# Two layers of a hybrid decoder in fp32 precision on one core: a list scheduler's cost model and priorities are changed

## The chip, the cores and the metric

One core of a Trainium2 chip. The time is that of one execution on the device, in microseconds (us); a run is given by the median of its executions. TensorE multiplies matrices into PSUM (8 banks), VectorE, ScalarE and GpSimd work on SBUF tiles, and SP issues all DMAs. In rows of the profile PE is TensorE (PEld its weight loads), DVE is VectorE, ACT is ScalarE, POOL is GpSimd, and SPq is the queue of SP.

## The reference

Two layers over x of 512 tokens by 1024 channels, float32. In each layer one input projection feeds four mixers, whose outputs (256 channels each) go through one output projection; then a LayerNorm, an MLP and a second LayerNorm.

```python
for l in range(DEPTH):                       # 2
    h = x @ w_in[l]
    (a_qkv, a_a, a_b, a_z, b_cq, b_ckv, b_kr, c_q, c_f, c_i, c_g, d_qkv) = split(h)
    o_a = _gated_deltanet(...)     # A: conv, L2 norm, chunks of 64, inverse of a unit triangular
                                   #    matrix per chunk, a state carried over 8 chunks, gated RMSNorm
    o_b = _mla(...)                # B: low-rank q and kv (RMSNorm), rotary key, causal softmax
    o_c = _hgrn2(...)              # C: forget gates, cumulative decays, outer-product state
    o_d = _dilated_attention(...)  # D: causal softmax with a bias table per head
    mixed = concat([o_a, o_b, o_c, o_d]) @ w_out[l]
    x = _layer_norm(ALPHA * x + mixed, ln1_g[l], ln1_b[l])
    x = _layer_norm(ALPHA * x + square(relu(x @ w_ff1[l])) @ w_ff2[l], ln2_g[l], ln2_b[l])
```

## The kernel before, in words

Everything stays transposed (channels on partitions, 512 tokens along the free dimension). A dense product is done in three TensorE matmuls of a reduced fp32 format (`mm3`): each operand is split into a high part (ScalarE, `split`) and the rest (VectorE), and high x high, high x low and low x high are added in PSUM. Weights come by DMA as `wr` (128x1024), and `wh` and `wl` are their two parts; activations are `xH`/`xL`, the mixers' outputs `mixH`/`mixL`, the MLP's `hH`/`hL`. A tile of the input projection is 24 dense matmuls of 512 columns. Small products (chunks of A and C, scores, transposes) are plain fp32 and use a part of the array: 64x64, 64x32, 32x32, 128x64 or 64x128 rows by columns of weights. Each such matmul leaves two records in the trace, a transpose one.

The program is written stage by stage, and each stage has a stream name: A, A0 and A1 (the two head pairs of A), B, C, C0 and C1, D, O (output projection, `w_out`, in three groups of mixer outputs) and F (MLP). Nothing is issued as it is written. `Plan.record` takes each instruction with its engine, what it depends on (`deps`, with a flag for a true read after write), a cost from `cost`, its tiles and a priority: its place in the program, less `bias`, plus `BIAS` of its stream and engine. `Plan.order` is a list scheduler: it keeps a clock per engine, and takes again and again the instruction that can start soonest by these costs; of those on one engine that can start equally soon the one of the lowest priority number. TensorE has more rules: it models the granted clock from its own activity (`WINDOW`, `DOWN`, `UP`), a price for leaving and entering a tile shape (`LEAVE`, `ENTER`), and it prefers dense matmuls while a running mean of activity (`EMA`) lies under `FILL`. Tiles are taken from pools of fixed size (41 rows of 128x512, 8 PSUM banks, 2 `wr`, 5 `wh`, 5 `wl`); `wr`, `wh` and `wl` go in the order of the program, and the dense accumulators (`mm`) hold at most 5 banks. `emit` then issues the instructions in that order, engine by engine; all have the line of `emit`'s loop, L472.

Names that the steps speak of. A: `LT` is the triangular matrix, `X`, `LB`, `W` and `TB` the steps of its inverse (15 pairs of `W` and `TB`, each pair reading the last), `Z` and then `U` and `T` the inverse put back by transposes; `a<-T,N` is TensorE's first use of it. `ke` and `ktok` are keys in token order, `vn` and `st` the state. B: `sqh`/`sql` are the two parts of a square whose sum over channels TensorE takes, `qh`/`kh` queries and keys, `at`/`as` the softmax of one head, `btab` its table. C: `kr`, `qa`, `sc`, `kt`, `vt`, `sn`. D: `dq`, `dk` and `dl` (high and low parts), `dtab` its four tables; its softmax is `at`/`as` too, and `tt` the transposed result. O: `xt` are the eight tiles of x, loaded before the first group (`load_x`) and added to on VectorE.

## Time and profile before

| | us |
|---|---|
| median of three runs | 1382.39 |
| lowest, highest | 1381.54, 1384.11 |
| the profiled execution | 1383.82 |
| its span, first to last instruction | 1382.0 |
| mean granted TensorE clock | 0.985 |
| TensorE, VectorE, ScalarE, GpSimd busy | 1336.3, 784.7, 596.6, 91.4 |

The span is what the page and the trace show; the execution takes 1.8 us more. A busy TensorE is not TensorE at its peak: its matmuls overlap, and the ends of their records are modelled, so the time from start to start is what a matmul costs in a row of them. A granted clock of 1.00 is 2.4 GHz, 0.50 is 1.2 GHz. The two layers lie at 0 to 690 us and 690 to 1382 us; in each, the mixers take the first half and the MLP the second.

### The profile page before, as it was taken

To read this page: it belongs to the slowest core of one execution; us is meant where nothing else is said; L and a number is where in the kernel's file an instruction comes from. 1 tells how busy PE (TensorE), PEld (TensorE's weight loads), DVE (VectorE), ACT (ScalarE), POOL (GpSimd) and SP (SyncE) were. 2 spreads that over 40 slices of the span, in tenths; PEclk is the share of its full clock that TensorE was granted. 3 is DMA by queue.
4 is the path that set the end of the run, shared out by engine and by line. 5 is a ranking of instruction groups with operands and counts; after the bars stand their busy time and mean duration, and the time that the engine had idled before them with its cause. 6 is when DMAs were issued, how large, how long until landed. Compare 5 with 4: busy or idle time off the path is not lost.

```text
span 1382.0 us, 21797 instructions
## 1 busy us (share of the span) xinstructions
PE 1336.3 (97%) x8860; PEld 1084.0 (78%) x8860; DVE 784.7 (57%) x1533; ACT 596.6 (43%) x1124; POOL 91.4 (7%) x108
## 2 busy tenths in 40 slices
PE   8899999999999999999998989999999999999997
PEld 7657778778888888888886678787788888888886
DVE  6989585567743334422479898846658333344226
ACT  6643456548432223321485434656374322233112
POOL 0222020010000000000003212200000000000000
PEclk9999999999999999999999999999999999999999
DMA  6122201232542223324122242021415323232341
GB/s 225 40 88 77 82 4 47 77 122 74 165 141 93 92 92 94 105 92 155 59 92 62 92 146 71 3 69 69 135 64 189 116 92 92 92 106 92 126 149 61
DMA packets 44164, 132.65 MB, mean 96 GB/s; under 512 B 4896, under 2 KB 5152, under 8 KB 44064
## 3 DMA queue, kind: packets, MB, share of 16 engines
q1 hardware_dynamic: 44064, 131.27, 29.5%
q8 instruction: 69, 1.13, 0.3%
q14 instruction: 31, 0.25, 0.1%
HBM read 122.86 MB, written 8.39 MB: 95 GB/s over the span
## 4 chain that ended last, share of the span: by engine, by line
PE 76%; DVE 14%; ACT 7%; issue 2%; DMA 1%; POOL 0%; SPq 0%; DVEq 0%; POOLq 0%; ACTq 0%
PE mm L472 42%; PE a L472 17%; PE b L472 16%; ACT lny L472 2%; DVE wl L472 1%; DVE xt L472 1%; DVE y L472 1%; ACT wh L472 1%; DVE vtok L472 1%; PE o L472 1%; DVE ktok L472 1%; ACT scr L472 1%; ACT sg L472 1%; ACT xH L472 1%; DVE X L472 1%
## 5 line engine op out<-in xcount | busy, mean ns | idle before, releaser
L472 DVE TENSOR_TENSOR wl<-wr,wh 128x1024 fp32r<-128x1024 f32 (+1 forms) x195 | 237.6, 1222 | 360.4 <-ACT wh L472 355.1
L472 ACT ACTIVATE wh<-wr 128x1024 fp32r<-128x1024 f32 (+1 forms) x195 | 204.7, 1054 | 528.6 <-PE mm L472 501.1
L472 PE MATMUL mm<-xH,wl 128*128 128x512 f32 (+1 forms) x832 | 328.0, 395 | 0.0
L472 PE MATMUL mm<-xL,wh 128*128 128x512 f32 (+1 forms) x832 | 326.6, 393 | 0.0
L472 PE MATMUL mm<-xH,wh 128*128 128x512 f32 (+1 forms) x832 | 325.7, 392 | 0.7 <-DVE as L472 0.4
L472 PEld LDWEIGHTS mm<-xH,wh 128*128 128x128 f32 x832 | 157.9, 190 | 38.1 <-issue 1.9
L472 PEld LDWEIGHTS mm<-xL,wh 128*128 128x128 f32 x832 | 157.5, 190 | 38.1 <-issue 2.3
L472 PEld LDWEIGHTS mm<-xH,wl 128*128 128x128 f32 x832 | 157.6, 190 | 34.8 <-issue 1.6
L472 DVE TENSOR_TENSOR hL<-h,hH 128x512 fp32r<-128x512 f32 x64 | 41.8, 687 | 73.4 <-PE mm L472 73.2
L472 PE MATMUL b<-wh,hL 128*128 128x512 f32 x192 | 74.8, 390 | 0.0
L472 PE MATMUL b<-wh,hH 128*128 128x512 f32 x192 | 74.8, 390 | 0.0
L472 PE MATMUL a<-wh,hH 128*128 128x512 f32 x192 | 74.8, 389 | 0.0
L472 PE MATMUL a<-wl,hH 128*128 128x512 f32 x192 | 74.8, 389 | 0.0
L472 PE MATMUL b<-wl,hH 128*128 128x512 f32 x192 | 74.7, 389 | 0.0
L472 PE MATMUL a<-wh,hL 128*128 128x512 f32 x192 | 74.7, 389 | 0.0
L472 PE MATMUL mm<-wh,hH 128*128 128x512 f32 x128 | 49.9, 390 | 0.0
L472 PE MATMUL mm<-wh,hL 128*128 128x512 f32 x128 | 49.8, 389 | 0.0
L472 PE MATMUL mm<-wl,hH 128*128 128x512 f32 x128 | 49.8, 389 | 0.0
L472 ACT ACTIVATE at<-at,as 128x512 f32<-128x512 f32 (+3 forms) x64 | 35.7, 558 | 27.6 <-DVE as L472 27.5
L472 ACT ACTIVATE hH<-h 128x512 fp32r<-128x512 f32 x64 | 37.3, 619 | 15.4 <-DVE h L472 15.2
L472 DVE TENSOR_TENSOR h<-h,mm 128x512 f32<-128x512 f32 x60 | 40.6, 680 | 3.6 <-ACT h L472 3.6
L472 PEld LDWEIGHTS a<-wl,hH 128*128 128x128 f32 x192 | 36.1, 188 | 7.6
(292 smaller groups left out, 2275.8 us busy)
## 6 DMA issues: line engine op xcount, KB each, us to landing
wr<-in_w_ff_dram SPq DMA_DIRECT2D x128, 512.0 KB, 3.6
wr<-in_w_in_dram SPq DMA_DIRECT2D x47, 512.0 KB, 3.6
wr<-in_w_out_dram SPq DMA_DIRECT2D x16, 512.0 KB, 3.6
x<-xt SPq DMA_DIRECT2D x24, 256.0 KB, 2.1
xt<-x SPq DMA_DIRECT2D x24, 256.0 KB, 5.8
ln<-in_ln_dram SPq DMA_DIRECT2D x16, 256.0 KB, 5.5
x<-in_xT_dram SPq DMA_DIRECT2D x8, 256.0 KB, 6.1
dtab<-in_tabs_dram SPq DMA_DIRECT2D x8, 256.0 KB, 4.0
```

Source lines behind the costliest of these rows:

```text
L472: getattr(e.real, method)(*[real(v) for v in a], **{n: real(v) for n, v in k.items()})
```

## The change

Only the planner and its numbers change; every instruction, tile and pool stays (the built programs hold the same instructions on each engine), and their order moves. The planner now:

- knows reads in place: `ins` keeps an operand that is also the output, so a chain of in-place steps on one engine has its latency;
- blocks VectorE and GpSimd against each other (`shares`, `PORT`) where a GpSimd instruction reads SBUF and a VectorE one reads two SBUF operands, or is a copy or tensor_scalar from SBUF to SBUF;
- knows which of the 16 squares of 32x32 of the array a matmul uses (`cells`), lets the next matmul start as soon as its own squares are free, and pays for a change of shape from the moment that the array is empty (`drained`);
- counts the activity behind its model of the clock by the rows of the array and the columns streamed (`streaming`), with other bounds, and has other values of `FILL`, `EMA` and `BURST`;
- has 23 priorities by stream and engine in place of 4.

```diff
 BIGS = 5
 RESERVE = {"row": 0, "ps": 0}
 FIFO = ("wr", "wh", "wl")
-FILL = (0.3, 0.5)
-EMA = 2000.0
-BURST = 2
+FILL = (0.2, 0.30000000000000004)
+EMA = 3000.0
+BURST = 3
 PATIENCE = 2000.0
 DENSE = 0.8
-BIAS = {('A0', 'ac'): -50, ('B', 've'): 600, ('C0', 've'): 200, ('D', 'ac'): -200}
+BIAS = {('', 've'): -50, ('A0', 'ac'): 100, ('A0', 'po'): -150, ('A1', 'ac'): -275, ('A1', 'po'): 25,
+        ('B', 'po'): 75, ('B', 've'): 600, ('C', 'pe'): -50, ('C', 'po'): 200, ('C', 've'): 25,
+        ('C0', 'ac'): 1200, ('C0', 'pe'): 100, ('C0', 'po'): -1175, ('C0', 've'): 200, ('C1', 'ac'): 750,
+        ('C1', 'pe'): -200, ('C1', 'po'): 600, ('D', 'ac'): -600, ('D', 'pe'): 400, ('D', 've'): 175,
+        ('F', 'ac'): 100, ('F', 'pe'): 25, ('O', 'ac'): 775}
 GROUPS = ((2, 3), (4, 5), (0, 1, 6, 7))
 WBIAS = 0
 OBIAS = 400
...
     HOP = {"pe": 197.0, "ac": 145.0, "ve": 128.0, "po": 103.0, "sy": 100.0}
     TO_PE = 70.0
+    ISSUE = 6.0
+    PORT = 100.0
     LEAVE, ENTER = 95.0, {(128, 128): 105.0}
-    WINDOW, DOWN, UP = 3413.0, 0.29, 0.65
+    WINDOW, DOWN, UP = 3413.0, 0.36, 0.38
     def __init__(self, nc):
         self.nc, self.ops, self.tiles = nc, [], 0
         self.kinds, self.queues, self.stream, self.bias = {}, {}, "", 0
         self.quota, self.reserve, self.fifo = {}, {}, set()
-        self.ties, self.tied = {}, None
+        self.ties, self.tied, self.streams = {}, None, []
     @contextmanager
     def together(self):
...
             if w.dt == FR:
                 return max(n * 0.4167 + 13.5, 109.0)
             t = 2 * max(2 * n * 0.4167 + 3, 2 * min(m, n) * 0.4167 + 3, 25.0)
-            if w.shape[0] <= 64 or m <= 64:
-                return t - 12 if out.span()[0] < 64 else 12.0
             return t
         if e == "ve":
             if method == "transpose":
...
             return 190 + 2.2 * n
         return 450.0
+    def shares(self, e, method, ins, out):
+        inside = [v for v in ins if v.buf.kind != "ps"]
+        if e == "po":
+            return bool(inside)
+        if e != "ve":
+            return False
+        return len(inside) > 1 or (method in ("tensor_scalar", "tensor_copy") and len(inside) == 1 and out.buf.kind != "ps")
     def tile_of(self, method, k):
         if method == "transpose":
             return (128, 128)
...
             return None
         grid = lambda c: 32 if c <= 32 else 64 if c <= 64 else 128
         return grid(k["lhsT"].shape[0]), grid(k["lhsT"].shape[1])
+    def cells(self, method, a, k):
+        if method == "transpose":
+            return tuple(range(16))
+        rows, cols = self.tile_of(method, k)
+        r, c = k["lhsT"].span()[0] // 32, a[0].span()[0] // 32
+        return tuple(4 * i + j for i in range(r, r + rows // 32) for j in range(c, c + cols // 32))
+    def streaming(self, e, method, k):
+        if e.name != "pe":
+            return 0.0
+        if method == "transpose":
+            return 107.0
+        w, n = k["lhsT"], math.prod(k["rhs"].shape[1:])
+        return n * 0.4167 * (1 if w.dt == FR else 4) * w.shape[0] / 128
     def activity(self, e, method, k, cost):
...
             outs.append(a[7])
         if isinstance(k.get("accum_out"), View):
             outs.append(k["accum_out"])
-        ins = [v for v in [*a[1:], *k.values()] if isinstance(v, View) and not any(v is o for o in outs)]
+        ins = [v for v in [*a[1:7], *(v for w, v in k.items() if w not in ("out", "accum_out"))] if isinstance(v, View)]
         if method == "copy_predicated" or (method == "matmul" and not k["start"]):
             ins.append(out)
         outs = [v for v in outs if isinstance(v, View)]
...
             b.uses += 1
         if self.tied is not None and e.name == "pe":
             self.tied.append(i)
+        self.streams.append(self.stream)
         self.ops.append([e, method, a, k, deps, list(bufs.values()), cost, tail, i + self.bias + BIAS.get((self.stream, e.name), 0),
-                         self.activity(e, method, k, cost), self.tile_of(method, k)])
+                         self.activity(e, method, k, cost), self.tile_of(method, k), self.shares(e.name, method, ins, out),
+                         self.cells(method, a, k) if e.name == "pe" else (),
+                         self.streaming(e, method, k)])
     def order(self):
         ops = self.ops
...
         held = {}
         last = {}
         dma_at = win = busy = ema = 0.0
-        warm, dense, mode, run, forced = False, True, None, 0, None
+        warm, dense, mode, run, forced, ports = False, True, None, 0, None, {"ve": 0.0, "po": 0.0}
+        free, drained = [0.0] * 16, 0.0
         self.warm = [True] * n
         result = []
         self.start = [0.0] * n
...
                 pick = None
                 for i in cand if forced is None or e != "pe" else (forced,):
                     t = max(at[e], ready[i])
+                    if ops[i][11]:
+                        t = max(t, ports["po" if e == "ve" else "ve"])
                     new = [b for b in ops[i][5] if not b.held]
                     if new:
                         room = {}
...
                         for kd, c in room.items():
                             t = max(t, sorted(slots[kd])[c - 1])
                     turn = e == "pe" and mode is not None and ops[i][10] != mode
+                    if e == "pe":
+                        t = max(t, drained) if turn else max(t, max(free[c] for c in ops[i][12]))
                     if turn and at[e] - ready[i] < PATIENCE:
                         t += self.LEAVE
                     key = (t, e == "pe" and (dense or 0 < run < BURST) and ops[i][9] < DENSE, ops[i][8])
...
             _, i, new, e = best
             op = ops[i]
             t = max(at[e], ready[i])
+            if op[11]:
+                t = max(t, ports["po" if e == "ve" else "ve"])
             for kd in {b.kind for b in new}:
                 t = max(t, sorted(slots[kd])[sum(b.kind == kd for b in new) - 1])
             for b in new:
...
                 work = cost * op[9]
                 if not warm:
                     cost, work = 2 * cost, 2 * work
+                busy += op[13]
                 if mode is not None and op[10] != mode:
-                    t = max(t, at[e] + self.LEAVE)
+                    t = max(t, drained + self.LEAVE)
                     cost += self.ENTER.get(op[10], 50.0)
+                else:
+                    t = max(t, max(free[c] for c in op[12]))
+                self.start[i] = t
                 mode, forced = op[10], self.ties.get(i)
                 run = run + 1 if op[9] >= DENSE else 0
-                busy += work
-                gap = math.exp(-(t - at[e]) / EMA)
+                gap = math.exp(-max(0.0, t - drained) / EMA)
                 keep = math.exp(-cost / EMA)
                 ema = ema * gap * keep + work / cost * (1 - keep)
                 dense = not warm or ema < (FILL[1] if dense else FILL[0])
-            at[e] = t + cost
+            at[e] = end[i] = t + cost
+            if op[11]:
+                ports[e] = at[e] - self.PORT
             self.warm[i] = warm
-            end[i] = at[e]
+            if e == "pe":
+                drained = max(drained, end[i])
+                for c in op[12]:
+                    free[c] = end[i]
+                if len(op[12]) < 16:
+                    at[e] = t + self.ISSUE
             if op[7]:
                 dma_at = max(dma_at, t + 500) + op[7] - 2000
                 end[i] = dma_at + 1800
...
                     lat = 0.0
                 else:
                     lat = self.HOP[e] + (self.TO_PE if dst == "pe" else 0.0)
-                ready[j] = max(ready[j], end[i] + lat)
+                ready[j] = max(ready[j], (t if dst == e == "pe" else end[i]) + lat)
                 if not need[j]:
                     avail[ops[j][0].name].append(j)
             for b in op[5]:
```

**VectorE, layer one, the end of the inverse, up to the transposes that give `T`.** Before:

```order
L472 TENSOR_TENSOR TB<-TB,W 128x2x14
L472 TENSOR_TENSOR wl<-wr,wh 128x1024
L472 TENSOR_TENSOR W<-LB,TB 128x15
L472 TENSOR_TENSOR TB<-TB,W 128x15
L472 TENSOR_SCALAR Z<-TB,cc 128x16x16 x3
L472 STREAM_TRANSPOSE U<-Z 32x16x2x16 x4
L472 TENSOR_SCALAR Z<-TB,cc 128x16x16
L472 TENSOR_TENSOR wl<-wr,wh 128x1024
L472 STREAM_TRANSPOSE T<-Z 32x16x2x16 x4
```

Now, at the same place:

```order
L522 TENSOR_TENSOR TB<-TB,W 128x2x14
L522 TENSOR_TENSOR W<-LB,TB 128x15
L522 TENSOR_TENSOR TB<-TB,W 128x15
L522 TENSOR_SCALAR Z<-TB,cc 128x16x16 x3
L522 STREAM_TRANSPOSE U<-Z 32x16x2x16 x4
L522 TENSOR_SCALAR Z<-TB,cc 128x16x16
L522 STREAM_TRANSPOSE vt<-ci 32x8x32
L522 STREAM_TRANSPOSE T<-Z 32x16x2x16 x4
```

One `wl` is gone from ahead of `T` and one transpose `vt` has come; further up, between earlier pairs of `W` and `TB`, the softmax of two heads of B now stands there. (L522 is the line of `emit`'s loop in the changed kernel.)

**TensorE, layer one, the scores of D** (`a<-dk,dq` and `a<-dk,dl` are the two parts of a score; `mm` with `mixH`, `mixL` is the output projection). Before:

```order
L472 MATMUL a<-dk,dq 128x512 x4
L472 MATMUL a<-dk,dq 128x384 x4
L472 MATMUL a<-dk,dl 128x512 x4
L472 MATMUL a<-dk,dl 128x384 x4
L472 MATMUL a<-dk,dq 128x256
L472 MATMUL a<-dk,dl 128x256
L472 MATMUL a<-dk,dq 128x256
L472 MATMUL a<-dk,dl 128x256
```

Now, at the second of these matmuls:

```order
L522 MATMUL mm<-wh,mixL_2605 128x512
L522 MATMUL mm<-wh,mixH_2643 128x512
L522 MATMUL a<-dk,dl 128x512
L522 MATMUL mm<-wh,mixH_2643 128x512
L522 MATMUL mm<-wl,mixH_2643 128x512
L522 MATMUL mm<-wh,mixL_2653 128x512
L522 MATMUL mm<-wh,mixH_2593 128x512
L522 MATMUL mm<-wl,mixH_2593 128x512
L522 MATMUL mm<-wh,mixL_2605 128x512
L522 MATMUL mm<-wl,mixH_2643 128x512
L522 MATMUL mm<-wh,mixL_2653 128x512
L522 MATMUL mm<-wh,mixH_2593 128x512
```

The block of D's scores is broken up, and the matmuls of the output projection's first two groups stand between its pieces.

**SP, layer one, the loads before and in the output projection** (`xt` is x, `dtab` are D's tables). Before:

```order
L472 DMA wr<-in_w_out_dram 128x1024 x3
L472 DMA dtab<-in_tabs_dram 128x512
L472 DMA wr<-in_w_out_dram 128x1024
L472 DMA dtab<-in_tabs_dram 128x512 x3
L472 DMA wr<-in_w_out_dram 128x1024 x3
L472 DMA xt<-in_x_dram 128x512 x8
L472 DMA wr<-in_w_out_dram 128x1024
```

Now:

```order
L522 DMA wr<-in_w_out_dram 128x1024 x5
L522 DMA xt<-in_x_dram 128x512 x8
L522 DMA wr<-in_w_out_dram 128x1024 x2
L522 DMA dtab<-in_tabs_dram 128x512 x4
L522 DMA wr<-in_w_out_dram 128x1024
```

x moved ahead of two of the weights and of D's tables.

## Rows read from the trace of the kernel before

**Rows 1.** The page: busy time by engine, and the chain that ended last.
```profile
PE 1336.3 (97%) x8860; PEld 1084.0 (78%) x8860; DVE 784.7 (57%) x1533; ACT 596.6 (43%) x1124; POOL 91.4 (7%) x108
...
PE 76%; DVE 14%; ACT 7%; issue 2%; DMA 1%; POOL 0%; SPq 0%; DVEq 0%; POOLq 0%; ACTq 0%
```

**Rows 2.** Busy time by stage (stretch: length, PE, PEld, DVE, ACT, POOL, clock, DMA, GB/s).
```profile
42.00:133.00 91.00, 81.38 (x433) 59.09 (x432) 85.37 (x165) 41.64 (x66) 26.86 (x28) 0.94 0.24 75
133.00:217.00 84.00, 81.00 (x1512) 63.76 (x1509) 61.40 (x165) 40.85 (x111) 13.33 (x19) 0.99 0.12 35
...
342.00:690.00 348.00, 347.95 (x1591) 287.01 (x1590) 136.93 (x183) 113.48 (x171) 0.00 (x0) 1.00 0.34 109
...
735.00:837.00 102.00, 93.56 (x672) 69.86 (x671) 93.65 (x172) 41.57 (x66) 26.58 (x26) 0.93 0.30 99
```

**Rows 3.** Who TensorE waited for (us in total, times, longest us).
```profile
PE a L472 <- DVE sql L472: 7.7, 4, 3.1
PE a L472 <- DVE T L472: 7.0, 4, 2.0
...
PE mm L472 <- DVE xt L472: 3.4, 3, 1.6
PE a L472 <- DVE as L472: 3.0, 4, 1.0
PE b L472 <- DVE qh L472: 2.9, 1, 2.9
```

**Rows 4.** Busy time in stretches at half clock (columns as in rows 2).
```profile
63.60:70.40 6.80, 5.68 (x12) 3.64 (x12) 6.77 (x10) 0.00 (x0) 2.20 (x2) 0.50 0.22 77
128.40:135.30 6.90, 5.75 (x108) 5.75 (x109) 4.89 (x11) 2.25 (x3) 0.00 (x0) 0.51 0.01 3
258.10:261.60 3.50, 3.50 (x12) 2.74 (x11) 3.46 (x18) 2.12 (x7) 0.00 (x0) 0.51 0.02 9
...
814.50:821.30 6.80, 5.01 (x67) 4.61 (x66) 5.84 (x8) 1.82 (x3) 0.00 (x0) 0.50 0.65 197
...
944.20:947.60 3.40, 3.40 (x14) 2.90 (x13) 3.40 (x16) 2.12 (x7) 0.00 (x0) 0.50 0.02 5
```

**Rows 5.** The chain in order of time, a dense run (start, us, what).
```profile
359.45 156.80 PE mm L472 x672
```

**Rows 6.** Timeline of TensorE: first use of `T`, scores of B.
```profile
127.44 0.33 PE L472 MATMUL a<-T,N 64*64 64x64 f32 x2 [1.39 <-DVE T L472]
...
164.59 2.84 PE L472 MATMUL a<-kh,qh 128*128 128x512 f32 x6
```

**Rows 7.** Groups of VectorE's instructions (busy us, mean ns | idle before).
```profile
L472 DVE TENSOR_TENSOR wl<-wr,wh 128x1024 fp32r<-128x1024 f32 x191 | 233.8, 1228 | 358.7 <-ACT wh L472 353.6 <-DMA xt<-x 4.2
...
L472 DVE STREAM_TRANSPOSE vt<-ci 32x256 f32<-32x256 f32 x32 | 13.9, 436 | 2.4 <-ACT ci L472 1.9
...
L472 DVE TENSOR_SCALAR at<-at,as 128x512 f32<-128x512 f32 x16 | 8.3, 535 | 0.1
...
L472 DVE TENSOR_TENSOR ke<-ktok,ce 128x512 f32<-128x512 f32 x4 | 7.0, 1761 | 0.0
...
L472 DVE CUSTOM_DVE_ANT_0 at<-a,btab 128x512 f32<-128x512 f32 x8 | 5.3, 684 | 0.1
```

**Rows 8.** Timeline of TensorE, D's scores in layer one (start us, us, what, wait before).
```profile
254.08 0.38 PE L472 MATMUL a<-dk,dq 128*128 128x256 f32 x1 [0.98 <-DVE as L472]
254.40 0.38 PE L472 MATMUL a<-dk,dl 64*128 64x256 f32 x1
...
256.59 0.38 PE L472 MATMUL a<-dk,dq 128*128 128x256 f32 x1 [0.56 <-DVE as L472]
...
257.70 0.50 PE L472 MATMUL mm<-xH,wh 128*128 128x512 f32 x1 [0.41 <-DVE as L472]
```

**Rows 9.** Timeline of SP, the loads before the output projection of layer one.
```profile
253.62 34.50 SPq L472 DMA_DIRECT2D wr<-in_w_out_dram  x3
288.21 4.05 SPq L472 DMA_DIRECT2D xt<-in_x_dram  x8
```

## The prediction

> **What bounds the kernel now.** I read the page first, then the busy times by stage, then who waited for whom, then the granted clock, and the timeline at the places that these name. TensorE shows busy for 1336.3 us of the span, and the chain that ended last is 76% TensorE and 14% VectorE [rows 1]. So a change of order alone can only win back what TensorE loses: waits, stretches at the lower clock, and changes of the array's tile shape. The stages tell where that is [rows 2]. From 342 to 690 us (feed-forward) TensorE is busy for 347.95 of 348.00 us at full clock: nothing is to be had. From 42 to 133 us VectorE is busy for 85.37 of 91.00 us, and it is the same in the second layer (93.65 of 102.00): there VectorE sets the pace, and TensorE loses 8 to 10 us per layer plus clock. From 133 to 217 us TensorE is busy for 81.00 of 84.00 us, VectorE for 61.40: TensorE sets the pace again.
>
> TensorE's waits name the places [rows 3]: 7.7 us for `sql` (the sums of the B stage), 7.0 for `T` (the triangular inverse), 3.4 for `xt` (the loaded x, before the output projection), 3.0 for `as` (softmax of D), 2.9 for `qh`. Five of the stretches at half the full clock (granted 0.50 or 0.51, so the 1.2 GHz level of 1.2 and 2.4) begin in or right behind such waits [rows 4]: 63.6 and 128.4 us at `sql` and `T`, 814.5 at the second layer's `T`, 258.1 and 944.2 behind D's scores.
>
> **The change part by part.** No instruction is added or removed; the planner's costs, its view of in-place reads and the priorities move them. Head (to 42 us), feed-forward and the end keep nearly their order, so they count as nothing.
>
> *1. Work put ahead of the wait for `T`.* Counted over the two TensorE orders, 25 dense matmuls of C's projections and two of B's score matmuls (four records) now stand ahead of the first `a<-T,N` of layer one, and 22 dense ones in layer two. A dense one takes 156.80 / 672 = 0.233 us where nothing is waited for [rows 5]. Six score records of B take 2.84 us with the drain of the last [rows 6], so 0.43 each for four. That is 25 x 0.233 + 4 x 0.43 = 7.5 us, and 22 x 0.233 = 5.1 us. VectorE decides when `T` comes, so what it does ahead of `T` counts against this. Layer one gains two softmax heads of B and one transpose ahead of `T`, and loses one `wl`: 2 x 0.684 + 2 x 0.535 + 0.436 - 1.228 = +1.6 us [rows 7]; with the two reciprocals and accumulator reads on one column I take +2.1. Layer two loses one `wl` and one `TENSOR_SCALAR` like the `at` one: -1.228 - 0.535 = -1.8. So when `T` is there, TensorE is further on by 7.5 - 2.1 = 5.4 and 5.1 + 1.8 = 6.9 us: **-12.3 us**. There is room for it: the waits for `sql`, `qh` and `T` alone are 17.6 us, and the half-clock stretch at 63.6 us, TensorE busy for 5.68 of it, lost 2.8 more. What follows from this view: the waits for `sql` and `qh` go, but a wait for `T` stays, since TensorE comes sooner to it and VectorE hardly sooner. So I count nothing for the half clock behind `T`. If the wait goes too, this term is larger by up to 7.0 us, and by half of the 6.90 and 6.80 us at 128.4 and 814.5, 6.9.
>
> *2. Changes of the array's tile shape.* By the shapes of their weights, the two TensorE orders change tile shape 189 times before and 159 times now. The price is read where D's scores alternate between 128-row and 64-row weights: start to start 0.32 us (254.08 to 254.40, [rows 8]) for a 256-column matmul whose own share is half of a dense 0.233, so 0.2 us per change. 30 x 0.2 = **-6.0 us**, most of it in the stages 133 to 217 us and its twin, where TensorE sets the pace. Ends: nothing, if only the 64-row matmul of such a pair is slow or if the engine waits there anyway, and 6.0; I take 6.0, the one price that a row gives.
>
> *3. D among the output projection.* Before, the scores of D come in one block while dense work is queued behind them: two waits of 0.98 and 0.56 us and one of 0.41 at the dense matmul [rows 8], in the second layer alike; the scores' waits are 3.0 us in all [rows 3], with the dense one 3.4. Behind each block the clock is at half for 3.50 and 3.40 us with TensorE busy all the time [rows 4]: half of it is lost, 3.4 us. Now single scores stand among matmuls of the output projection, with several dense ones between a score and its transposes. That cover is 3 to 12 dense matmuls, 0.7 to 2.8 us, so the waits go, and so should the fall of the clock: **-6.8 us**. What covers them is the output projection's own work; if that is late, both come back (rival below).
>
> *4. The lock between VectorE and GpSimd.* `ke` takes 1761 ns for 128x512, where another VectorE instruction of that size takes 684 [rows 7]; GpSimd works beside it. In the new orders the same four `ke` and the same GpSimd instructions stand in the same stages, some pairs exchanged, so by the row I count zero. Ends: four times 1.08, 4.3 us gained, or as much lost where a new pair meets. The Trainium skill, "SBUF — State Buffer", section SBUF: two separate sides, says that the shared port pair is an exclusive lock and the loser stands still for the whole instruction, whoever starts first. The trace agrees in kind, 1761 ns against 684. By that rule the order alone decides who stands still, so a planner that knows it could take all of the 4.3 us out, and the time would be 1353.
>
> The sum: 12.3 + 6.0 + 6.8 = 25.1 us. The profiled execution took 1383.8 us (span 1382.0), 1.4 above the median of the runs, 1382.4; so 1383.8 - 25.1 = 1358.7 for such an execution and **1357.3** for the median.
>
> **The rivals.** *Only part is kept.* If the stage behind `T` (133 to 217 us) is not set by TensorE but by the chain of C, what was put ahead of `T` is waited for later. For it: C's two halves change places, so the half that comes last now has its `kt` and `sn` steps closer to the end, and VectorE's 61.40 us there are not few. Against: TensorE's 81.00 of 84.00 [rows 2]. Then term 1 falls away and half of 2: 1382.4 - 6.8 - 3.0 = 1372.6.
>
> *More than the sum.* VectorE comes sooner to `T` because the planner fills the gaps between dependent in-place steps and sets GpSimd apart. Then the wait for `T`, the half clock behind it and the lock go too: 1357.3 - 7.0 - 6.9 - 4.3 = 1339.1. Against: VectorE is busy for 94% of that stage already.
>
> *It does nothing that can be measured*: 1382.4. The planner's clock and quarters are only guesses at the chip, and what one wait gives another takes. A measurement of this kernel tells 0.2%, 2.8 us, from no change. For it speaks only that `T` bounds both versions; against, that terms 2 and 3 don't depend on `T`.
>
> *Slower: the loads of x.* SP issues in order. Before, the eight loads of x were issued at 288.21 us, behind three loads of `w_out` that took SP 34.50 us to issue [rows 9], and TensorE waited 3.4 us for them in all [rows 3]. Now x stands behind five `w_out` loads instead of seven and the four D tables behind it, but the first output matmuls stand ahead of nearly all of D's scores. Those began by 254.1 us [rows 8]; until 288.2 TensorE had 34.1 us, of which the last 48 dense matmuls of stage A (11.2 us, now earlier) are taken off: 22.9 us of D's work stood ahead of the output projection that now stands behind it. If x comes no sooner than it did, TensorE waits up to 22.9 us in each layer, and D waits behind it: 1357.3 + 45.8 = 1403. It decides from a wait of 12.5 us per layer on. Against: two of the seven `w_out` loads no longer stand ahead, and those were most of SP's 34.50 us.
>
> **How the numbers follow.** Terms as counted, with a few us either way (1345 to 1368): 0.50. Only part: 0.22. More: 0.10. Nothing: 0.06. Slower by x: 0.12. The time is that of the likeliest, 1357. What the two ends of the lock's price give lies inside its 1345 to 1368. Faster by over 0.2% are the first three, 0.82; same 0.06; slower 0.12. Low end: the third case, 1338. High end: up to the fourth, 1381, which leaves the slower case and part of "nothing" above, some 0.16, and 0.03 below.
>
> **What would show it right or wrong.** In the profile after: TensorE's waits for `sql` and `qh` gone or under 1 us each, a wait for `T` still there in both layers (3 us or more in all) with half clock behind it; no wait for `as` among D's scores and no half clock in the stage of the output projection; a wait for `xt` of a few us, not tens; pairs of alternating D scores gone. The first term is wrong if TensorE's first `a<-T,N` (at 127.44 us before, [rows 6]) comes more than 2 us later, or if it is no longer waited for at all; the second if the stage 133 to 217 us does not become shorter; the third if a half-clock stretch shows between D's first score and the end of the output projection.

## The result and the profile after

The changed kernel takes 1348.4 us, the kernel before 1382.6 (medians of four runs each); the ratio is 0.9754, 95% interval 0.9731 to 0.9777. Forecast were 1357, between 1338 and 1381. The profiled execution took 1346.8 us (span 1345.0), 37.0 less than the profiled one of before; the granted clock is 0.996 in place of 0.985. Of the changed kernel's four executions two have a clock of 0.996 and two of 0.993 and 0.994, so the profile is of one with little time at half clock.

The page, busy time by engine and the chain that ended last (before: [rows 1]):

```profile
PE 1315.1 (98%) x8860; PEld 1067.9 (79%) x8860; DVE 773.1 (57%) x1533; ACT 593.7 (44%) x1124; POOL 90.5 (7%) x108
...
PE 82%; ACT 8%; DVE 7%; issue 1%; DMA 1%; POOL 0%; DVEq 0%; SPq 0%; ACTq 0%; POOLq 0%
```

VectorE's share of the chain has fallen from 14% to 7%, and its busy time by 11.6 us, though it runs the same instructions.

Who TensorE waited for:

```profile
PE a L522 <- ACT wh L522: 5.2, 1, 5.2
PE a L522 <- DVE T L522: 5.0, 2, 4.8
PE a L522 <- DVE sql L522: 2.2, 1, 2.2
PE a L522 <- DVE xt L522: 1.4, 4, 0.4
...
PE a L522 <- DVE as L522: 0.8, 1, 0.8
```

Against [rows 3], `qh` is gone, `sql` has fallen from 7.7 to 2.2, `as` from 3.0 to 0.8, and no output matmul (`mm`) waits for `xt` any more (the `xt` here are transposes of the layer norm). `T` is down from 7.0 to 5.0, and nearly all of it is one wait in layer two. All rows of this view together come to 37.7 us before and 21.9 now.

Of the seven stretches at half clock ahead of the program's last microseconds, 37.5 us in all (five of them in [rows 4]; the others at 753.1 and 879.4 us), one is left, behind that wait; busy times in it (columns as in [rows 2], the clock is the 0.51):

```profile
798.90:805.70 6.80, 4.14 (x65) 3.99 (x66) 6.48 (x13) 3.07 (x6) 2.20 (x6) 0.51 0.56 213
```

The chain in order of time, the dense run of the feed-forward (start, us, what); first the kernel before, layer two (layer one is [rows 5]), then the changed kernel, both layers:

```profile
1043.51 156.80 PE mm L472 x672
```
```profile
335.82 156.81 PE mm L522 x672
...
1006.50 156.80 PE mm L522 x672
```

Layer one reaches it 359.45 - 335.82 = 23.6 us sooner, layer two 37.0, so 13.4 of its own; what follows takes as long as before. To see where, I split each layer at TensorE's first `a<-T,N` (the change put 7.5 and 5.1 us of work ahead of it, as counted in the prediction). Its timeline there, layer two before, then both layers now (layer one before is in [rows 6]):

```profile
814.27 0.33 PE L472 MATMUL a<-T,N 64*64 64x64 f32 x2 [2.05 <-DVE T L472]
```
```profile
124.68 2.08 PE L522 MATMUL a<-T,N 64*64 64x64 f32 x64
...
788.31 0.33 PE L522 MATMUL a<-T,N 64*64 64x64 f32 x2
```

| | layer one | layer two |
|---|---|---|
| first `a<-T,N`, before and now | 127.44, 124.68 | 814.27, 788.31 |
| earlier by, without what layer one gave | 2.8 | 2.3 |
| with the work put ahead | 10.3 | 7.4 |
| from there to the feed-forward, before and now | 232.0, 211.1 | 229.2, 218.2 |
| gained there, without the work put ahead | 13.4 | 5.9 |

The one long wait for `T` that is left, 4.8 us in layer two, lies behind the first `a<-T,N`: it is in the 5.9, and the 7.4 is counted without it.

VectorE, layer one, timeline of the pairs `W` and `TB` (start us, us, what), the kernel before:

```profile
106.42 1.30 DVE L472 TENSOR_TENSOR TB<-TB,W 128x55 f32<-128x55 f32 x1
...
110.50 1.22 DVE L472 TENSOR_TENSOR TB<-TB,W 128x63 f32<-128x63 f32 x1
...
125.31 4.20 DVE L472 STREAM_TRANSPOSE T<-Z 32x512 f32<-32x512 f32 x4
```

and now:

```profile
105.30 0.21 DVE L522 TENSOR_TENSOR TB<-TB,W 128x55 f32<-128x55 f32 x1
...
107.18 0.22 DVE L522 TENSOR_TENSOR TB<-TB,W 128x63 f32<-128x63 f32 x1
...
119.79 4.39 DVE L522 STREAM_TRANSPOSE T<-Z 32x512 f32<-32x512 f32 x4
```

The same instructions took 1.30 and 1.22 us and now take 0.21 and 0.22. `T` is complete at 124.2 us, 5.3 sooner than before. GpSimd, timeline, before and now:

```profile
105.19 2.46 POOL L472 TENSOR_TENSOR fl<-fl,fe 128x512 f32<-128x512 f32 x1 [21.39 <-ACT fe L472]
...
110.34 1.30 POOL L472 TENSOR_TENSOR fl<-fl,fe 128x512 f32<-128x512 f32 x1
```
```profile
85.53 1.29 POOL L522 TENSOR_TENSOR fl<-fl,fe 128x512 f32<-128x512 f32 x1
...
89.94 1.28 POOL L522 TENSOR_TENSOR fl<-fl,fe 128x512 f32<-128x512 f32 x1 [0.18 <-ACT fe L522]
```

Before, C's forget gates `fl` ran on GpSimd in the midst of the inverse; now they are done before its long pairs begin. The group of `ke` shows the same (before 1761 ns, [rows 7]):

```profile
L522 DVE TENSOR_TENSOR ke<-ktok,ce 128x512 f32<-128x512 f32 x4 | 3.8, 960 | 0.0
```

Two of VectorE's groups by shape, before and now:

```profile
L472 DVE TENSOR_TENSOR W<-LB,TB 128x63 f32<-128x63 f32 x4 | 3.0, 752 | 0.1
L472 DVE TENSOR_TENSOR TB<-TB,W 128x63 f32<-128x63 f32 x4 | 2.1, 521 | 0.1
```
```profile
L522 DVE TENSOR_TENSOR W<-LB,TB 128x63 f32<-128x63 f32 x4 | 2.0, 497 | 0.1
L522 DVE TENSOR_TENSOR TB<-TB,W 128x63 f32<-128x63 f32 x4 | 0.9, 226 | 0.1
```

There are the same four instructions in each. The mean of `TB` more than halves; that of `W` falls less, because one of its four, in layer two at 769.8 us, still takes 1.32 us. I counted this over all of VectorE: an instruction is drawn out if it takes over 0.15 us more than the tenth percentile of its operation and shape over all the traces of this case. Before, 38 were, by 22.3 us in all; now 18, by 11.1 us (these sums move by 1 to 3 us with how the shapes are grouped). In every trace of this case each of them overlaps a GpSimd instruction in time; of VectorE's 1533 instructions only 156 to 190 do.

### The profile page after: what moved, and what is told of

Read it like the earlier page. It is cut to its first block, busy times and chain, and to the rows that moved or that the text cites. A ratio compares the mean times of both kernels' runs of the same rounds, so it can differ in the third digit from the quotient of the medians.

```text
span 1345.0 us, 21767 instructions
## 1 busy us (share of the span) xinstructions
PE 1315.1 (98%) x8860; PEld 1067.9 (79%) x8860; DVE 773.1 (57%) x1533; ACT 593.7 (44%) x1124; POOL 90.5 (7%) x108
## 4 chain that ended last, share of the span: by engine, by line
PE 82%; ACT 8%; DVE 7%; issue 1%; DMA 1%; POOL 0%; DVEq 0%; SPq 0%; ACTq 0%; POOLq 0%
PE mm L522 46%; PE a L522 18%; PE b L522 16%; ACT lny L522 2%; PE o L522 2%; ACT wh L522 1%; DVE xt L522 1%; DVE wl L522 1%; ACT xH L522 1%; DVE ktok L522 1%; DMA wr<-in_w_in_dram 1%; ACT sg L522 1%; DVE kt L522 1%; ACT scr L522 0%; DMA ln<-in_ln_dram 0%
## 5 line engine op out<-in xcount | busy, mean ns | idle before, releaser
L522 DVE TENSOR_TENSOR wl<-wr,wh 128x1024 fp32r<-128x1024 f32 (+1 forms) x195 | 239.4, 1232 | 341.9 <-ACT wh L522 327.2
L522 ACT ACTIVATE wh<-wr 128x1024 fp32r<-128x1024 f32 (+1 forms) x195 | 204.9, 1055 | 499.3 <-PE mm L522 442.8
L522 PE MATMUL mm<-xH,wl 128*128 128x512 f32 (+1 forms) x832 | 325.1, 392 | 0.3 <-DVE wl L522 0.3
L522 PE MATMUL mm<-xL,wh 128*128 128x512 f32 (+1 forms) x832 | 322.0, 388 | 0.2
L522 PE MATMUL mm<-xH,wh 128*128 128x512 f32 (+1 forms) x832 | 322.2, 389 | 0.0
L522 PEld LDWEIGHTS mm<-xH,wh 128*128 128x128 f32 x832 | 156.1, 188 | 38.0 <-issue 3.5
L522 PEld LDWEIGHTS mm<-xL,wh 128*128 128x128 f32 x832 | 156.4, 188 | 37.3 <-issue 1.3
L522 PEld LDWEIGHTS mm<-xH,wl 128*128 128x128 f32 x832 | 156.3, 188 | 35.3 <-issue 1.5
L522 DVE TENSOR_TENSOR hL<-h,hH 128x512 fp32r<-128x512 f32 x64 | 41.8, 689 | 73.2 <-PE mm L522 73.2
L522 PE MATMUL b<-wh,hH 128*128 128x512 f32 x192 | 74.9, 390 | 0.0
L522 PE MATMUL a<-wl,hH 128*128 128x512 f32 x192 | 74.7, 389 | 0.0
L522 PE MATMUL a<-wh,hH 128*128 128x512 f32 x192 | 74.7, 389 | 0.0
L522 PE MATMUL b<-wh,hL 128*128 128x512 f32 x192 | 74.7, 389 | 0.0
L522 PE MATMUL b<-wl,hH 128*128 128x512 f32 x192 | 74.7, 389 | 0.0
L522 PE MATMUL a<-wh,hL 128*128 128x512 f32 x192 | 74.7, 389 | 0.0
L522 PE MATMUL mm<-wh,hH 128*128 128x512 f32 x128 | 49.9, 390 | 0.0
L522 PE MATMUL mm<-wh,hL 128*128 128x512 f32 x128 | 49.8, 389 | 0.0
L522 PE MATMUL mm<-wl,hH 128*128 128x512 f32 x128 | 49.8, 389 | 0.0
L522 ACT ACTIVATE at<-at,as 128x512 f32<-128x512 f32 (+3 forms) x64 | 35.6, 562 | 21.8 <-DVE as L522 21.5
L522 DVE TENSOR_TENSOR h<-h,mm 128x512 f32<-128x512 f32 x60 | 40.9, 682 | 4.6 <-ACT h L522 4.6
L522 ACT ACTIVATE hH<-h 128x512 fp32r<-128x512 f32 x64 | 37.4, 618 | 13.2 <-DVE h L522 13.0
L522 PEld LDWEIGHTS b<-wh,hH 128*128 128x128 f32 x192 | 36.1, 188 | 7.5
```

The source lines that it names most:

```text
L522: getattr(e.real, method)(*[real(v) for v in a], **{n: real(v) for n, v in k.items()})
```

## The experiments

All ratios are to the kernel before, timed on the same chip; the changed kernel's own is 0.9754. "Half clock" is the length of all such stretches but the program's last one, "drawn out" VectorE's sum as above.

| run | us | ratio (95%) | waits | half clock | drawn out |
|---|---|---|---|---|---|
| before | 1382 | 1 | 37.7 | 37.5 | 22.3 |
| the change | 1348.4 | 0.9754 (0.9731 to 0.9777) | 21.9 | 6.8 | 11.1 |
| e1 model, old priorities | 1378.5 | 0.9981 (0.9966 to 0.9996) | 37.8 | 30.7 | 13.1 |
| e2 priorities, old model | 1381.0 | 0.9996 (0.9988 to 1.0005) | 28.5 | 37.5 | 23.4 |
| e3 without the lock | 1359.9 | 0.9850 (0.9835 to 0.9865) | 28.4 | 23.9 | 19.6 |
| e4 without reads in place | 1372.9 | 0.9939 (0.9923 to 0.9955) | 35.9 | 44.4 | 15.2 |
| e5 without quarters | 1363.5 | 0.9869 (0.9851 to 0.9887) | 19.7 | 6.8 | 13.7 |
| e6 old count of the clock | 1349.1 | 0.9762 (0.9747 to 0.9777) | 21.6 | 6.8 | 10.8 |
| e7 norm's tail late | 1344.1 | 0.9729 (0.9714 to 0.9743) | 15.9 | 0 | 10.7 |
| e8 D's priorities back | 1353.0 | 0.9790 (0.9776 to 0.9804) | 27.0 | 20.5 | 10.9 |
| e9 GpSimd work added | 1353.3 | 0.9792 (0.9779 to 0.9805) | 23.2 | 10.2 | 14.1 |
| e10 old FILL, EMA, BURST | 1374.2 | 0.9945 (0.9933 to 0.9957) | 29.5 | 20.5 | 11.5 |
| c1 priorities jittered | 1358.6 | 0.9830 (0.9817 to 0.9843) | 24.3 | 20.5 | 13.0 |
| c2 hops 5% longer | 1375.7 | 0.9960 (0.9943 to 0.9976) | 29.3 | 44.4 | 11.7 |

### Model and priorities apart

The first is the changed kernel with

```diff
-FILL = (0.2, 0.30000000000000004)
-EMA = 3000.0
-BURST = 3
-BIAS = {('', 've'): -50, ('A0', 'ac'): 100,
...
+FILL = (0.3, 0.5)
+EMA = 2000.0
+BURST = 2
+BIAS = {('A0', 'ac'): -50, ('B', 've'): 600, ('C0', 've'): 200, ('D', 'ac'): -200}
```

> The changed planner, with the 4 old priorities and the old FILL, EMA and BURST; 181 changes of tile shape in TensorE's order (159 in the changed kernel, 189 before), 104.6 us of TensorE work ahead of the first use of T in layer one (106.2 and 98.8). If the model carries the gain (it knows where a VectorE and a GpSimd instruction meet): 1350 to 1360, VectorE's drawn-out instructions near the 10.6 us of the changed kernel and far from the 21.2 of before. If the priorities carry it: 1370 or more, and the block of D's scores in one piece again.

The second is the kernel before with the 23 new priorities in place of its 4, nothing else.

> The kernel before, with the 23 new priorities alone; 200 changes of tile shape, 98.8 us of TensorE work ahead of the first use of T in layer one. If the priorities carry the gain: 1350 to 1360. If they only fit the new model: 1375 to 1390, VectorE's drawn-out instructions at 20 us or so as before.

Neither is faster by more than 0.2%: 3 us and 1 us, where both together give 34. Neither carries the gain. In e1 VectorE's drawn-out time is near the changed kernel's (13.1 and 11.1), as the planner's lock should have it, but TensorE's waits are as before and the half clock nearly; layer one reaches the feed-forward at 347.46 us, 12.0 sooner, and layer two then loses 7.0 again.

### One piece of the model out

```diff
     def shares(self, e, method, ins, out):
 
+        return False
```

> The changed kernel, whose planner no longer blocks VectorE and GpSimd against each other; 99.9 us of TensorE work ahead of the first use of T (106.2 with it), 152 changes of tile shape. My theory now, that the lock was worth much more than the nothing I counted: VectorE's drawn-out instructions go from 10.6 us back to 18 or more, some of them in the chain of the inverse, T comes 4 us or so later in each layer and the time is 1355 to 1362. Rival, the lock plays no part and the gain is TensorE's order alone: 1346 to 1351.

As the theory had it: 11.5 us slower, 19.6 us drawn out, and `T` is complete at 127.7 us in layer one, 3.5 later than with the change. VectorE's timeline in layer one has drawn-out pairs again:

```profile
109.40 1.31 DVE L523 TENSOR_TENSOR W<-LB,TB 128x63 f32<-128x63 f32 x1
110.74 0.54 DVE L523 TENSOR_TENSOR TB<-TB,W 128x63 f32<-128x63 f32 x1
```

Next, the line that keeps an operand that is also the output is put back to the old one:

```diff
-        ins = [v for v in [*a[1:7], *(v for w, v in k.items() if w not in ("out", "accum_out"))] if isinstance(v, View)]
+        ins = [v for v in [*a[1:], *k.values()] if isinstance(v, View) and not any(v is o for o in outs)]
```

> The changed kernel, whose planner again does not see reads in place; 152 changes of tile shape, 105.6 us of work ahead of T (106.2). If it matters, the planner packs the 15 pairs W and TB of the inverse as if they had no latency, VectorE idles or runs other work late, T comes 1 to 3 us later in each layer: 1350 to 1355. Rival, it does nothing: 1346 to 1351.

Missed: 24.6 us slower, the most of the four pieces, and not where I looked. The state `st` of A is updated in place too; TensorE's waits are now in the chain `st`, `vn`, `ot` of the eight chunks:

```profile
PE a L522 <- DVE vn L522: 4.6, 10, 1.2
...
PE a L522 <- DVE st L522: 4.3, 8, 1.1
PE a L522 <- ACT ot L522: 3.3, 8, 0.4
```

Busy times in the two longest stretches at half clock, which lie there, one in each layer (in all there are 44.4 us of it, 37.6 more than with the change; at most half of that, 18.8, is lost):

```profile
161.60:175.30 13.70, 11.95 (x122) 7.90 (x118) 1.74 (x6) 1.01 (x6) 1.25 (x4) 0.51 0.05 17
857.90:871.60 13.70, 10.02 (x118) 8.00 (x115) 5.02 (x20) 3.60 (x13) 0.80 (x2) 0.51 0.00 1
```

The profiled execution is the slowest of six, 1378.1 us at a granted clock of 0.983; the others have 0.984 to 0.989, so less time at half clock.

Then every small matmul takes the whole array (`cells` returns all 16 squares, the old cost of the second half of the rows is back):

```diff
+        return tuple(range(16))
         rows, cols = self.tile_of(method, k)
...
+            if w.shape[0] <= 64 or m <= 64:
+                return t - 12 if out.span()[0] < 64 else 12.0
             return t
```

> The changed kernel, whose planner takes each small matmul as the whole array again (and the old cost of a matmul in the second half of the rows); 195 changes of tile shape in place of 159, 107.4 us of work ahead of T. By the second term, 36 changes at 0.16 to 0.2 us give 5.8 to 7.2: 1354 to 1356 if the rest holds. Rival, the planner's view of the whole array sets the order of the chain of A and C apart from the changes of shape: 1360 or more, with waits for vn, st, as or ot of several us each, as in the run with the old priorities. Rival, nothing: within 3 us of 1348.

15.1 us slower, so neither 36 changes of shape alone nor nothing. The time is that of the first rival, but its sign, long waits, is missing: waits (19.7 us) and half clock (6.8) are not worse than with the change. What the waits don't list is lost between small matmuls. Measured from start to start of TensorE's records, against the mean spacing of the same matmul at full clock in all traces of this case, what lies outside waits, changes of shape and half clock takes some 11 us more here than with the change, and the changes of shape some 6 more.

Then the planner counts the clock's activity as before (`work` in place of `op[13]`), with the old bounds:

```diff
-    WINDOW, DOWN, UP = 3413.0, 0.36, 0.38
+    WINDOW, DOWN, UP = 3413.0, 0.29, 0.65
...
-                busy += op[13]
...
+                busy += work
```

> The changed kernel, whose planner counts the clock's activity as before and with the old bounds; 159 changes of tile shape as in the changed kernel, the work ahead of T the same. If the planner's picture of the clock matters, stretches at half clock come back, two or more of 3.4 or 6.8 us, at 1.7 to 3.4 us each: 1352 to 1358. Rival, the clock follows from the waits and those from the order, and the planner's picture of it does little: 1346 to 1351.

The rival holds: 0.7 us, well inside both intervals. The planner's new picture of the clock gives nothing that these runs can tell, though TensorE's order is another one here.

### The priorities of D

```diff
-        ('C1', 'pe'): -200, ('C1', 'po'): 600, ('D', 'ac'): -600, ('D', 'pe'): 400, ('D', 've'): 175,
-        ('F', 'ac'): 100, ('F', 'pe'): 25, ('O', 'ac'): 775}
+        ('C1', 'pe'): -200, ('C1', 'po'): 600, ('D', 'ac'): -200,
+        ('F', 'ac'): 100, ('F', 'pe'): 25}
```

> The changed kernel with the priorities of D and of ScalarE's O as they were (D on ScalarE -200 in place of -600, none for D on TensorE and VectorE and for O on ScalarE); 143 changes of tile shape. By the third term of the prediction the block of D's scores comes back in one piece, with some 3 us of waits for as and 3 us of half clock: 1353 to 1357. Rival: the new model alone breaks the block up, and what the priorities of D give is elsewhere or nothing: 1344 to 1351.

4.6 us slower, at the edge of what the third term gives. The block is back (first to last score 21 us in place of 56 in layer one), with its waits, in the list of TensorE's:

```profile
PE a L522 <- DVE as L522: 3.3, 4, 1.0
```

and half clock among its scores in each layer (busy times):

```profile
239.30:242.70 3.40, 3.18 (x8) 2.45 (x8) 2.78 (x13) 2.48 (x8) 0.00 (x0) 0.53 0.22 86
911.80:918.60 6.80, 6.71 (x16) 4.72 (x16) 6.76 (x28) 4.85 (x16) 0.00 (x0) 0.51 0.34 127
```

The waits of the output matmuls for `xt` are back as well, 2.5 us: x is issued at 266.6 us here, behind D's tables and seven loads of `w_out` again, and at 240.9 us in the changed kernel.

### The lock by itself

The same order on every engine as in the changed kernel (but for two pairs of small matmuls that change places), and eight GpSimd instructions more, of which the planner knows no lock:

```diff
                 ve.tensor_copy(kh[2 * p + h][lo], o[half[h]])
+                kl = kh[2 * p + h][lo]
+                po.tensor_tensor(dm[lo], kl, kl, OP.mult)
+                plan.ops[-1][11] = False
```

> The changed kernel with the same order on every engine and eight GpSimd multiplications of 64x512 more, four in each layer: each reads a piece of kh that VectorE has just copied there and writes a tile that nobody reads, so that they run beside the pairs W and TB of the inverse. The lock by itself: if GpSimd's reads stand still VectorE, its drawn-out instructions grow from 11 us by 5 to 9 us, T comes 3 to 4 us later in layer one, TensorE waits for it again and the time is 1352 to 1360. If GpSimd beside VectorE costs nothing by itself (the drawn-out instructions have another cause): 1347 to 1350, and W and TB take 0.2 us each as they do.

The time is in the forecast, 4.9 us up; the drawn-out time grew by 3.0 only, not by 5. GpSimd and VectorE, timelines of layer one:

```profile
99.81 5.36 POOL L522 TENSOR_TENSOR dm<-kh 64x512 f32<-64x512 f32 x4 [5.55 <-DVE kh L522]
```
```profile
100.47 0.43 DVE L522 TENSOR_TENSOR W<-LB,TB 128x39 f32<-128x39 f32 x1
100.93 0.68 DVE L522 COPY kh<-b 64x512 f32<-64x512 f32 x1
101.54 0.47 DVE L522 TENSOR_TENSOR TB<-TB,W 128x39 f32<-128x39 f32 x1
102.05 0.69 DVE L522 COPY kh<-b 64x512 f32<-64x512 f32 x1
102.66 0.48 DVE L522 TENSOR_TENSOR W<-LB,TB 128x48 f32<-128x48 f32 x1
103.06 1.21 DVE L522 TENSOR_TENSOR wl<-wr,wh 128x1024 fp32r<-128x1024 f32 x1
104.20 1.04 DVE L522 TENSOR_TENSOR TB<-TB,W 128x48 f32<-128x48 f32 x1
```

`W` and `TB` of 0.2 us take 0.43 to 1.04 while `dm` runs; the copies from PSUM between them keep their 0.68. Each seems to stand until the other engine is through: `W` begins at 100.47 us and ends at 100.90, the `dm` beside it at 100.84; and the last `dm` takes 2.02 us in place of 1.03 beside a `wl` that keeps its 1.21. `T` is complete 1.7 us later, TensorE waits for it again (its timeline),

```profile
125.88 1.32 PE L522 MATMUL a<-T,N 64*64 64x64 f32 x37 [0.69 <-DVE T L522]
```

and layer one reaches the feed-forward 1.05 us later (336.87). Layer two loses 3.5 more; it has two more stretches of half clock, at 720.8 and 731.1 us, ahead of its added instructions, and TensorE waits 1.1 us for a `wl` at 774.4 us, right behind them. That the stretches follow from the first microsecond is argued, not shown, so the forecast time was met in part by another path than the one forecast.

### The wait that is left

In layer two, VectorE does the last steps of the layer norm before (`xt<-xt,ln`) just ahead of `T<-T,a`; its timeline in the changed kernel:

```profile
791.54 4.30 DVE L522 TENSOR_TENSOR xt<-xt,ln 128x512 f32<-128x512 f32 x7
796.00 4.91 DVE L522 TENSOR_TENSOR xt<-xt,ln 128x512 f32<-128x512 f32 x8 [0.16 <-DMA ln<-in_ln_dram]
800.82 0.69 DVE L522 TENSOR_TENSOR T<-T,a 128x512 f32<-128x512 f32 x1
```

and TensorE waits (its timeline):

```profile
801.56 1.97 PE L522 MATMUL a<-U,Y 64*64 64x64 f32 x32 [4.79 <-DVE T L522]
```

The edit, behind the inverse (`bias` is added to an instruction's place in the program, so a higher one puts it further back):

```diff
+        plan.bias = 600
         flush()
+        plan.bias = 0
```

> The changed kernel, with the last steps of the layer norm before (the 16 additions and 16 multiplications xt<-xt,ln of layer two) put 600 places further back in priority; 165 changes of tile shape. Theory: in layer two 9.2 us of these stand on VectorE just ahead of T<-T,a, TensorE waits 4.8 us for it and then runs 6.8 us at half clock, so both go and the time falls by 5 to 8 us, to 1340 to 1343. Rival: they stand in the way of C's or D's steps later, or free their tiles too late, and the time stays within 3 us of 1348 or grows.

4.3 us faster than the change by the medians, short of the 5 forecast; the two intervals of the ratios overlap a little (0.9731 to 0.9743), though all four times lie below all four of the change. In the profiled execution what was to go is gone. `T<-T,a` comes at 791.67 us (VectorE's timeline),

```profile
791.67 0.68 DVE L522 TENSOR_TENSOR T<-T,a 128x512 f32<-128x512 f32 x1
```

no wait for `T` is left in the list, and no half clock ahead of the last microseconds. That holds for two executions, 1342.5 us at a granted clock of 0.999; the other two took 1345.6 and 1345.7 at 0.996, so some half clock is left in those. By its median, 1344.1 us, this is the fastest of all.

### The priorities' numbers, and two controls

The changed kernel with the old `FILL`, `EMA` and `BURST`, the 23 priorities kept:

> The changed kernel with the old FILL, EMA and BURST (when TensorE prefers dense work), and the 23 new priorities kept; 213 changes of tile shape in place of 159. With the old priorities and these old numbers the new model took 1378.5. If these three numbers are what the new model needs: 1365 or more, 54 changes of shape at 0.16 us (8.6 us) among it. If the priorities are: 1348 to 1358.

25.8 us slower, in the first of the two forecasts, with waits in the chain of `vn` (4.2), `ot` (3.8) and `st` (3.5 us). Two controls take no knowledge away. One moves each of the 23 priorities by 10 or 20:

```diff
-BIAS = {('', 've'): -50, ('A0', 'ac'): 100,
+BIAS = {('', 've'): -60, ('A0', 'ac'): 80,
...
```

> A control: the changed kernel, each of the 23 priorities moved by 10 or 20 up or down by a fixed draw; 167 changes of tile shape, 104.6 us of work ahead of T. How much any small disturbance of the planner costs, when it takes none of its knowledge away. If the pieces taken out one by one were worth what those runs lost (24.6, 15.1 and 11.5 us): this one stays within 5 us, 1344 to 1353. If what they lost is that the numbers no longer fit the planner exactly: 1358 or more.

The other makes the planner's times between engines longer:

```diff
-    HOP = {"pe": 197.0, "ac": 145.0, "ve": 128.0, "po": 103.0, "sy": 100.0}
+    HOP = {"pe": 207.0, "ac": 152.0, "ve": 134.0, "po": 108.0, "sy": 105.0}
```

> A second control of the same kind: the planner's times from engine to engine (HOP) are all 5% longer, its knowledge and the priorities the same; 172 changes of tile shape, 109.1 us of work ahead of T. Worth of the pieces real: 1344 to 1353. Loss of an exact fit: 1358 or more.

10.2 and 27.3 us slower: as much as taking a piece out. So what e3, e4, e5 and e10 lost can't be put down to the piece as such; each found another order, and most of these are some 10 to 25 us worse than the one that this set of numbers gives. Not every one is: e6's is not. What c2 lost is mostly in one place, a stretch of 37.5 us at half clock (busy times):

```profile
154.20:191.70 37.50, 29.54 (x251) 18.92 (x246) 9.05 (x28) 7.43 (x23) 2.00 (x5) 0.50 0.11 33
```

Who TensorE waited for from 137 to 192 us of it:

```profile
PE a L522 <- DVE st L522: 3.8, 7, 1.0
PE a L522 <- ACT ot L522: 2.6, 6, 0.4
PE a L522 <- DVE vn L522: 2.4, 6, 0.4
```

The chain of A's state runs with little beside it, its waits of 0.4 us come again and again, and TensorE stays at half clock for 37.5 us. At most half of that, 18.8 us, is lost by the clock; that would be most of the 27.3.

## Why the prediction was right, and where not

**Direction and, in the main, the mechanism** were right: TensorE's waits and half clock went, the order alone did it. The gain was 34.2 us by the medians, where 25.1 were forecast.

The terms below are read from the two profiled executions, which are 37.0 us apart. By TensorE's records from start to start, against the mean spacing of the same matmul at full clock in all traces, some 16 us of that are waits of over 0.15 us, 13 are half clock, 4 are changes of shape, and 4 lie between matmuls of one shape. The prediction had no term for these last 4: it took the spacing of small matmuls as given. In e5, whose planner does not know the array's squares, 11 us are lost there.

**Term 1, work ahead of `T`: 12.3 forecast, 17.7 measured** (10.3 and 7.4 in the table). The counts hold; the term failed at VectorE. I let `T` come 2.1 us later in layer one by the instructions put ahead, and it came 5.3 sooner. So no wait for `T` is left there, nor the half clock behind it, which I had kept. By the prediction's own sign the term is wrong in layer one, and that part of the second rival came true in one layer of two. In layer two the forecast wait stayed, 5.0 us with half clock behind it, though behind another step than I thought (`T<-T,a`). `sql` was to fall under 1 us and stayed at 2.2.

**Term 4, the lock, counted as nothing: this is the step that failed.** I took the one group whose mean stood out, `ke`, for the whole of it, 4.3 us at most. The pairs `W` and `TB` were hidden in groups that mix many shapes; the view by shape has the 128x63 ones at 521 ns. In layer one ahead of `T` the drawn-out time fell by some 5 us (4.4 to 5.5, by how the shapes are grouped), of the 7.4 by which I was off; the rest stays open. In the whole program the new order gave VectorE 11.2 us back; of these only what TensorE waits for is worth TensorE's time. The Trainium skill, "SBUF — State Buffer", section SBUF: two separate sides, has a condition that I passed over: besides some faster modes, the lock takes in VectorE instructions with two SBUF inputs, against a GpSimd instruction that reads SBUF. The runs agree: 0.43 to 1.04 us for `W` and `TB` beside `dm`, 0.68 as ever for copies from PSUM. Of the planner's pieces the lock's own effect is shown most directly: 19.6 to 23.4 us drawn out in the three kernels without it, 10.7 to 15.2 in the eleven with it.

**Terms 2 and 3, 12.8 forecast; behind `T`, where they lie, 19.3 measured.** By the split above, 7.5 us of these are half clock, 4.3 waits (the 4.8 us wait for `T<-T,a` stands against them), 3.5 changes of shape, and 3.9 lie between matmuls of one shape. So the count of term 2 holds, 189 and 159, but its price was too high: where no wait ends at it and the clock is full, a change costs some 0.12 us in either kernel. The 0.2 was read at D's scores alone. All changes together gave some 4 us for the forecast 6.0. D's share is 4.6 by e8, for 6.8, and no clean price, as the controls cost more than that. The sum behind `T` is high by what had no term: the half clock outside D's scores, at 128.4, 814.5 and 879.4 us, some 4 us when what is left at 798.9 us is taken off, and the 3.9 between matmuls of one shape.

**The rivals.** Only part was kept: no, what was put ahead of `T` was kept and more came behind. Nothing: no. Slower by the loads of x: no output matmul waits for `xt` now; x moved ahead of two weights and of D's tables, and that was enough: in e8, where it stands behind them again, the waits are back. That the planner's clock is a guess at the chip and moves nothing by itself is borne out by e6 alone, 0.7 us.

**Left open.** How much each piece of the model is worth by itself. It takes model, priorities and `FILL` together, and two small disturbances cost 10.2 and 27.3 us. Nor does any run have the old model with numbers tuned for it, so it is not shown that the knowledge was needed, and not only a search for numbers.

## What to carry to other kernels

Before you price a change of order, look for instructions that take longer than others of their own shape, by shape and not by a group's mean: here 38 of them hid 22 us of VectorE's time. After it, look at the longest wait that is left and at what its engine did just ahead: one line there (e7) gave 4.3 us more by the medians. A gain found with a set of tuned numbers belongs to the set; a part taken out, or a control of 5%, tells what the set loses, not what the part is worth.

## What was not expected of the hardware

A short VectorE instruction pays for a long GpSimd one: 0.2 us became 1.30 beside `fl` of 128x512, and GpSimd's own `fl` took 2.46 us there in place of 1.29, behind a VectorE `wl` of 1.21. And a fall of the clock need not be short: in c2 it lasted 37.5 us on end, with TensorE busy for 29.54 of them, where the longest of before was 6.8.
